# Batch normalisation over 64 tiles: the first store split in two column parts, the second store queued behind it

## The chip, the cores and the metric

The kernel runs on one core of one Trainium2 chip. The metric is the device time of one execution in microseconds (us), the median of several runs; lower is better.

## The reference

The kernel computes a batch normalisation with given (running) statistics, in float32:

```python
def setup_inputs():
    n = 32; c = 256; h = 128; w = 128
    # x: (n, c, h, w); gamma, beta, running_mean, running_var: (c,)

def reference(x, gamma, beta, running_mean, running_var):
    eps = 1e-5
    # the four parameters reshaped to (1, c, 1, 1)
    return gamma * (x - mean) / np.sqrt(var + eps) + beta
```

Per channel this is one multiplication and one addition: out = x * scale + shift, with scale = gamma / sqrt(var + eps) and shift = beta - mean * scale. The input has 537 MB and so has the output. Each element is read from HBM once and written once.

## The kernel before

**Tiles.** The 256 channels are two blocks of 128, one channel per partition. A tile is one image and one channel block: 128 partitions x 16384 columns (128 x 128 pixels) of float32, 64 KB per partition, 8.39 MB in all. There are NT = 64 tiles. SBUF holds NBUF = 3 tile buffers; tile i lives in buffer i modulo 3, is loaded into it, computed in place, and stored from it.

**Engines.** SP issues all loads, ACT issues all stores, each on its own DMA queue (q1 is SP's and q10 is ACT's in the profile). Both queues run on the core's 16 DMA engines. In every tile VectorE (DVE) computes columns 0 to 14336 (VCOLS) and ScalarE (ACT) computes the last 2048. VectorE does its share in two instructions (L132): the first covers STEP = 2560 columns, the second the rest. In tile 0 the first covers 8192 columns, since tile 0 is loaded in two halves. In the last tile VectorE stops at column 9216 (VLAST) and ACT does the remaining 7168 columns.

**Semaphores.** `early` and `loaded[s]` say that a load has landed in a buffer, `stored[s]` that a store from buffer s has landed. A DMA adds 16 when it is complete. `vdone` counts VectorE's parts (two per tile), `adone` those of ACT (one per tile).

**Order on SP.** The first half of tile 0 (L90), the four parameter rows (L93), the second half of tile 0 (L97), then tiles 1 to 63 in full (L104). Before load i, from tile 3 on, SP waits until the buffer's previous tile has been stored (L103) and until VectorE has done the first part of tile i - 1, which in turn needs load i - 1 to have landed. So apart from the first three tiles there is one load in flight at a time.

**Order on VectorE.** Scale and shift from the parameters (L91 to L127), then the two parts of each tile as it lands.

**Order on ACT.** For each tile i: wait until VectorE has done both its parts (`vdone`), wait until store i - 1 has landed, compute ACT's columns (L143), issue store i (L156), which waits for the computation. So there is one store in flight at a time. This loop is written out by hand, and ACT's instructions run in this order:

```python
for i in range(last):
    nc.scalar.wait_ge(vdone, 2 * (i + 1))
    inst = scalar_part(i, VCOLS)
    if i:
        inst._wait_ge(stored[(i - 1) % NBUF], 16 * ((i - 1) // NBUF + 1))
    store(i)
```

The last tile is computed as soon as it lands and stored without a wait for the store before it.

Of the kernel before, what the change touches and what calls it, by code (L numbers as in the profile page):

```python
# [8 lines left out]
NBUF = 3  # L9
# [2 lines left out]

STEP = 2560
VCOLS = 14336
VLAST = 9216


@with_exitstack
def kernel(
    ctx: ExitStack,  # L20
    tc: tile.TileContext,
    x: bass.AP,
    gamma: bass.AP,
    beta: bass.AP,
    running_mean: bass.AP,
    running_var: bass.AP,
    out: bass.AP,
):
    nc = tc.nc
    eps = 1e-5  # L30
    f32 = mybir.dt.float32

    N, C, H, W = x.shape
    P = nc.NUM_PARTITIONS
    assert C % P == 0
    NCB = C // P
    HW = H * W
    NT = N * NCB
    B = 32
    NQ = P // B  # L40
    NE = 16
    NPAR = 4

    xr = x.rearrange("n (cb p) h w -> (n cb) p (h w)", p=P)
    outr = out.rearrange("n (cb p) h w -> (n cb) p (h w)", p=P)

    params = ctx.enter_context(tc.tile_pool(name="params", bufs=1))
    data = ctx.enter_context(tc.tile_pool(name="data", bufs=1))
    params.tile([P, PAD], f32, name="pad", tag="pad")
    bufs = [data.tile([P, HW], f32, name=f"t{s}", tag=f"t{s}") for s in range(NBUF)]  # L50
    rows = params.tile([B, NPAR * C], f32, name="rows", tag="rows")
    turned = params.tile([B, NPAR * C], f32, name="turned", tag="turned")
    par = params.tile([P, NPAR, NCB], f32, name="par", tag="par")
    eps_t = params.tile([P, 1], f32, name="eps_t", tag="eps")
    std_t = params.tile([P, NCB], f32, name="std_t", tag="std")
    rstd_t = params.tile([P, NCB], f32, name="rstd_t", tag="rstd")
    scale_t = params.tile([P, NCB], f32, name="scale_t", tag="scale")
    ms_t = params.tile([P, NCB], f32, name="ms_t", tag="ms")
    shift_t = params.tile([P, NCB], f32, name="shift_t", tag="shift")

    loaded = [tc.alloc_semaphore(f"loaded{s}") for s in range(NBUF)]
    stored = [tc.alloc_semaphore(f"stored{s}") for s in range(NBUF)]
    early = tc.alloc_semaphore("early")
    vdone = tc.alloc_semaphore("vdone")
    adone = tc.alloc_semaphore("adone")
    fetched = tc.alloc_semaphore("fetched")
    vec = tc.alloc_semaphore("vec")
    act = tc.alloc_semaphore("act")  # L70

    with tc.tile_critical():  # L72
        count = [0]

        def step(inst, sem=None, value=None):

            if sem is not None:
                inst._wait_ge(sem, value)
            elif count[0]:
                inst._wait_ge(vec, count[0])  # L80
            inst.then_inc(vec, 1)
            count[0] += 1
            return count[0]

        left, right = slice(0, HW // 2), slice(HW // 2, HW)
        last = NT - 1

        nc.sync.dma_start(out=bufs[0][:, left], in_=xr[0][:, left]).then_inc(early, 16)  # L90
        zeroed = step(nc.vector.memset(rows[:], 0.0))  # L91
        for r, ap in enumerate((running_var, gamma, beta, running_mean)):
            inst = nc.sync.dma_start(out=rows[0:NE, r * C : (r + 1) * C], in_=ap.partition_broadcast(NE))  # L93
            if r == 0:
                inst._wait_ge(vec, zeroed)
            inst.then_inc(fetched, 16)
        nc.sync.dma_start(out=bufs[0][:, right], in_=xr[0][:, right]).then_inc(loaded[0], 16)  # L97
        for i in range(1, NT):
            s, turn = i % NBUF, i // NBUF


            if turn:
                nc.sync.wait_ge(stored[s], 16 * turn)  # L103
            inst = nc.sync.dma_start(out=bufs[s][:], in_=xr[i]).then_inc(loaded[s], 16)  # L104
            if turn:
                inst._wait_ge(vdone, 2 * (i - 1) + 1)


        step(nc.vector.memset(eps_t[:], eps))  # L109
        step(nc.vector.transpose(out=turned[:], in_=rows[:]), fetched, 16 * NPAR)  # L110

        blocks = turned.rearrange("p (rc q b) -> p rc q b", q=NQ, b=B)
        flat = par.rearrange("p r cb -> p (r cb)")
        for q in range(NQ):
            placed = step(nc.vector.tensor_copy(out=flat[q * B : (q + 1) * B], in_=blocks[:, :, q, 0]))  # L115
        var_t, gamma_t, beta_t, mean_t = (par[:, r] for r in range(NPAR))
        nc.scalar.activation(  # L117
            out=std_t[:],
            in_=var_t,
            func=mybir.ActivationFunctionType.Sqrt,  # L120
            bias=eps_t[:],
            scale=1.0,
        )._wait_ge(vec, placed).then_inc(act, 1)
        step(nc.vector.reciprocal(out=rstd_t[:], in_=std_t[:]), act, 1)  # L124
        step(nc.vector.tensor_mul(out=scale_t[:], in0=gamma_t, in1=rstd_t[:]))  # L125
        step(nc.vector.tensor_mul(out=ms_t[:], in0=mean_t, in1=scale_t[:]))  # L126
        ready = step(nc.vector.tensor_sub(out=shift_t[:], in0=beta_t, in1=ms_t[:]))  # L127
        nc.vector.wait_ge(vec, ready)

        def vector_part(i, first, end):  # L130
            t, cb = bufs[i % NBUF], i % NCB
            return nc.vector.tensor_scalar(  # L132
                out=t[:, first:end],
                in0=t[:, first:end],
                scalar1=scale_t[:, cb : cb + 1],
                scalar2=shift_t[:, cb : cb + 1],
                op0=mybir.AluOpType.mult,
                op1=mybir.AluOpType.add,
            ).then_inc(vdone, 1)

        def scalar_part(i, first):
            t, cb = bufs[i % NBUF], i % NCB
            return nc.scalar.activation(  # L143
                out=t[:, first:],
                in_=t[:, first:],
                func=mybir.ActivationFunctionType.Identity,
                bias=shift_t[:, cb : cb + 1],
                scale=scale_t[:, cb : cb + 1],
            ).then_inc(adone, 1)

        def landed(i):
            return loaded[i % NBUF], 16 * (i // NBUF + 1)

        def store(i):
            s = i % NBUF
            nc.scalar.dma_start(out=outr[i], in_=bufs[s][:])._wait_ge(adone, i + 1).then_inc(stored[s], 16)  # L156

        vector_part(0, 0, HW // 2)._wait_ge(early, 16)
        vector_part(0, HW // 2, VCOLS)._wait_ge(*landed(0))
        for i in range(1, NT):  # L160
            vector_part(i, 0, STEP)._wait_ge(*landed(i))
            vector_part(i, STEP, VLAST if i == last else VCOLS)
        for i in range(last):
            nc.scalar.wait_ge(vdone, 2 * (i + 1))
            inst = scalar_part(i, VCOLS)
            if i:
                inst._wait_ge(stored[(i - 1) % NBUF], 16 * ((i - 1) // NBUF + 1))
            store(i)
        scalar_part(last, VLAST)._wait_ge(*landed(last))
        nc.scalar.wait_ge(vdone, 2 * NT)  # L170
        store(last)

        for s in range(NBUF):
            nc.sync.wait_ge(stored[s], 16 * ((NT - s + NBUF - 1) // NBUF))
# [30 lines left out]
```

## Time and profile before

| what | value |
|---|---|
| median of 3 runs | 2482.92 us (2482.25 to 2483.06) |
| the profiled execution's own time | 2482.82 us |
| its span, from the first to the last instruction | 2481.0 us |
| moved by DMA | 1073.85 MB, mean 433 GB/s over the span |
| VectorE parts of 2560 columns (L132) | mean 1.61 us |
| ACT's part of a tile (L143, 2048 columns) | mean 2.09 us |
| load, from issue to landing (L104) | median 37.0 us |
| store, from issue to landing (L156) | median 36.5 us |
| first landing: load 1, load 2 | 55.55 us, 86.94 us |
| store 0: issued, landed | 29.06 us, 72.42 us |

The profile is one execution, recorded by the hardware profiler. "Span" is the time between the first and the last instruction; all times within it are counted from its start. L132 is line 132 of the kernel before. A row of instructions names the line, the engine, the operation and the tile that it writes and reads; "[43.38 <-DMA out_dram<-t]" says that the engine stood idle for 43.38 us before it and that a store ended this. In the waits, "a <- b: total, times, longest" says how long a waited for b. The DMA view counts packets by the time at which they begin, by queue; a packet of a full tile is one row of 64 KB. The share of a short window can be above 100% as whole packets are counted where they begin.

### The profile page before, as it was taken

How to read it: one execution, taken by the hardware profiler on the slowest of the kernel's cores; microseconds unless marked ns; L12 is line 12 of the kernel's file. 1: busy time of each engine (PE TensorE's matmuls, PEld its weight loads, DVE VectorE, ACT ScalarE, POOL GpSimd, SP SyncE). 2: the span in 40 equal slices, each digit the busy share in tenths (PEclk: the TensorE clock that was granted, in tenths of full speed). 3: DMA queues.
4: the chain of work that ended last, by engine and by line, in shares of the span. 5: the costliest groups of instructions: out<-in, count | busy, mean ns of one | idle time of the engine just before them, and what ended most of it. 6: DMA issues, size and time to landing. Idle time of an engine off the chain costs nothing.

```text
span 2481.0 us, 516 instructions
## 1 busy us (share of the span) xinstructions
DVE 508.8 (21%) x139; ACT 139.8 (6%) x66; POOL 0.2 (0%) x4
## 2 busy tenths in 40 slices
DVE  2122121221212212122121221212212122121120
ACT  0000000000000000000000000000000000000001
POOL 0000000000000000000000000000000000000000
DMA  9999999999999999999999999999999999999999
GB/s 411 435 440 428 433 440 432 430 440 432 430 440 437 427 438 436 428 437 436 432 433 438 430 434 437 432 432 437 434 431 436 437 428 437 437 428 435 437 432 402
DMA packets 18708, 1073.85 MB, mean 433 GB/s; under 512 B 2128, under 2 KB 2192, under 8 KB 2192
## 3 DMA queue, kind: packets, MB, share of 16 engines
q1 hardware_dynamic: 9488, 536.94, 50.0%
q10 hardware_dynamic: 9216, 536.88, 49.9%
q14 instruction: 4, 0.03, 0.0%
HBM read 536.94 MB, written 536.87 MB: 433 GB/s over the span
## 4 chain that ended last, share of the span: by engine, by line
DMA 92%; DVE 4%; another core or an unknown queue 2%; ACT 0%; issue 0%; SPq 0%; DVEq 0%
DMA t<-in_x_dram 92%; DVE t L132 4%; ACT t L143 0%; SPq L93 0%; DVE rows L91 0%; DVE eps_t L109 0%; DVEq L200 0%; SPq L72 0%
## 5 line engine op out<-in xcount | busy, mean ns | idle before, releaser
L132 DVE TENSOR_SCALAR t<-t,scale_t,shift_t 128x11776 f32<-128x11776 f32 (+2 forms) x128 | 505.3, 3989 | 1928.8 <-DMA t<-in_x_dram 1928.7
L143 ACT ACTIVATE t<-t,shift_t,scale_t 128x2048 f32<-128x2048 f32 x64 | 138.2, 2159 | 2297.8 <-DMA out_dram<-t 2274.9
L110 DVE STREAM_TRANSPOSE turned<-rows 32x1024 f32<-32x1024 f32 x1 | 1.2, 1232 | 11.8 <-DMA rows<-in_running_mean_dram 11.8
L117 ACT ACT_TABLE_LOAD x1 | 1.3, 1283 | 0.9 <-SPq L72 0.9
L91 DVE MEMSET rows<- 32x1024 f32 x1 | 0.9, 912 | 1.2 <-SPq L72 1.2
L117 ACT ACTIVATE std_t<-par,eps_t 128x2 f32<-128x2 f32 x1 | 0.3, 295 | 14.0 <-DVE par L115 14.0
L115 DVE COPY par<-turned 32x8 f32<-32x8 f32 x4 | 0.6, 162 | 0.1
L124 DVE RECIPROCAL rstd_t<-std_t 128x2 f32<-128x2 f32 x1 | 0.2, 166 | 0.4 <-ACT std_t L117 0.4
L125 DVE TENSOR_TENSOR scale_t<-par,rstd_t 128x2 f32<-128x2 f32 x1 | 0.2, 162 | 0.0
L127 DVE TENSOR_TENSOR shift_t<-par,ms_t 128x2 f32<-128x2 f32 x1 | 0.2, 162 | 0.0
L126 DVE TENSOR_TENSOR ms_t<-par,scale_t 128x2 f32<-128x2 f32 x1 | 0.2, 160 | 0.0
L189 POOL MEMSET const-bfloat16-1.0<- 128x1 bf16 x1 | 0.1, 101 | 0.0
L189 POOL MEMSET const-uint8-127<- 128x1 uint8 x1 | 0.1, 101 | 0.0
L189 POOL MEMSET const-float32-0.0<- 128x1 f32 x1 | 0.1, 98 | 0.2 <-issue 0.2
L189 POOL MEMSET const-float32-1.0<- 128x1 f32 x1 | 0.1, 98 | 0.0
L109 DVE MEMSET eps_t<- 128x1 f32 x1 | 0.1, 59 | 0.1
## 6 DMA issues: line engine op xcount, KB each, us to landing
t<-in_x_dram SPq DMA_DIRECT2D x2, 4096.0 KB, 15.9
out_dram<-t ACTq DMA_DIRECT2D x64, 36.5
t<-in_x_dram SPq DMA_DIRECT2D x63, 37.0
rows<-in_running_var_dram SPq DMA_DIRECT2D x1, 16.0 KB, 11.1
rows<-in_gamma_dram SPq DMA_DIRECT2D x1, 16.0 KB, 10.9
rows<-in_beta_dram SPq DMA_DIRECT2D x1, 16.0 KB, 10.7
rows<-in_running_mean_dram SPq DMA_DIRECT2D x1, 16.0 KB, 10.6
```

The costliest lines, as they stand in the source:

```text
L91: zeroed = step(nc.vector.memset(rows[:], 0.0))
L109: step(nc.vector.memset(eps_t[:], eps))
L110: step(nc.vector.transpose(out=turned[:], in_=rows[:]), fetched, 16 * NPAR)
L115: placed = step(nc.vector.tensor_copy(out=flat[q * B : (q + 1) * B], in_=blocks[:, :, q, 0]))
L117: nc.scalar.activation(out=std_t[:], in_=var_t, func=mybir.ActivationFunctionType.Sqrt, bias=eps_t[:], scale=1.0,)._wait_ge(vec, placed).t ...
L124: step(nc.vector.reciprocal(out=rstd_t[:], in_=std_t[:]), act, 1)
L125: step(nc.vector.tensor_mul(out=scale_t[:], in0=gamma_t, in1=rstd_t[:]))
L126: step(nc.vector.tensor_mul(out=ms_t[:], in0=mean_t, in1=scale_t[:]))
L127: ready = step(nc.vector.tensor_sub(out=shift_t[:], in0=beta_t, in1=ms_t[:]))
L132: return nc.vector.tensor_scalar(out=t[:, first:end], in0=t[:, first:end], scalar1=scale_t[:, cb : cb + 1], scalar2=shift_t[:, cb : cb + 1 ...
L143: return nc.scalar.activation(out=t[:, first:], in_=t[:, first:], func=mybir.ActivationFunctionType.Identity, bias=shift_t[:, cb : cb + 1] ...
L189: nc = _bacc.Bacc("TRN2", target_bir_lowering=False, num_devices=1)
```

## The change

The store of tile 0 becomes two DMAs. Columns 0 to 2048 are stored as soon as VectorE's first instruction (columns 0 to 8192 of tile 0) is done; the other 14336 columns are stored where the whole tile was stored before, after ACT's part. The early DMA has its own semaphore, `opened`, and is issued by ACT ahead of its first part. SP waits for it before it loads tile 3 into the same buffer. ACT's part of tile 1 no longer waits for store 0 to land, so that store 1 may be queued while store 0 is still in flight. From tile 2 on nothing is changed.

```diff
+FIRST = 2048
...
+    opened = tc.alloc_semaphore("opened")
...
+            if i == NBUF:
+                nc.sync.wait_ge(opened, 16)
             if turn:
                 nc.sync.wait_ge(stored[s], 16 * turn)
             inst = nc.sync.dma_start(out=bufs[s][:], in_=xr[i]).then_inc(loaded[s], 16)
...
         def store(i):
             s = i % NBUF
-            nc.scalar.dma_start(out=outr[i], in_=bufs[s][:])._wait_ge(adone, i + 1).then_inc(stored[s], 16)
+            cols = slice(0 if i else FIRST, HW)
+            nc.scalar.dma_start(out=outr[i][:, cols], in_=bufs[s][:, cols])._wait_ge(adone, i + 1).then_inc(stored[s], 16)
...
+        nc.scalar.dma_start(out=outr[0][:, :FIRST], in_=bufs[0][:, :FIRST])._wait_ge(vdone, 1).then_inc(opened, 16)
         for i in range(last):
             nc.scalar.wait_ge(vdone, 2 * (i + 1))
             inst = scalar_part(i, VCOLS)
-            if i:
+            if i > 1:
                 inst._wait_ge(stored[(i - 1) % NBUF], 16 * ((i - 1) // NBUF + 1))
             store(i)
```

## The prediction

> **What bounds the kernel now.** First the page: busy shares and queues. Columns of the queue rows: packets, MB, share of the 16 DMA engines' time.
>
> ```profile
> span 2481.0 us, 516 instructions
> DVE 508.8 (21%) x139; ACT 139.8 (6%) x66; POOL 0.2 (0%) x4
> ...
> q1 hardware_dynamic: 9488, 536.94, 50.0%
> q10 hardware_dynamic: 9216, 536.88, 49.9%
> ```
>
> No engine is near busy; the loads (q1, issued by SP) and the stores (q10, issued by ACT) together fill the 16 DMA engines. Next, stretches of the span (start:end, length, busy times, clock, DMA share, GB/s):
>
> ```profile
> 0.00:1.95 1.95, 0.73 (x1) 1.05 (x1) 0.20 (x4) 1.00 0.00 0
> ...
> 60.00:2440.00 2380.00, 487.57 (x123) 129.73 (x62) 0.00 (x0) 1.00 1.00 434
> ...
> 2479.40:2481.00 1.60, 0.00 (x0) 0.00 (x0) 0.00 (x0) 1.00 0.00 0
> ```
>
> From 1.95 to 2479.4 us the engines never stand still. 1073.85 MB at the 434 GB/s of the middle are 2474 us, so out of 2481.0 only 7 us are anything else: 1.95 before the first packet, 1.6 after the last, some 3 of start-up. **Nothing that reorders these transfers can win more than that.** The question is only whether the new order keeps the engines full.
>
> That is read from the order of packets. A load or a full store is 128 rows of 64 KB, 8 on each engine. Three short windows of the DMA view, 83.6 to 93.2, 93.2 to 107.8 and 107.8 to 117.3 us:
>
> ```profile
> q10 hardware_dynamic: 64, 4.19, 100.8%
> q1 hardware_dynamic: 16, 0.00, 0.1%
> ...
> q1 hardware_dynamic: 48, 3.15, 49.7%
> q10 hardware_dynamic: 48, 3.15, 49.7%
> ...
> q1 hardware_dynamic: 64, 4.19, 101.8%
> q10 hardware_dynamic: 16, 0.00, 0.1%
> ```
>
> When both queues hold work each engine takes one packet of each in turn; the pair of a load and a store (16 packets per engine) comes round every 38.65 us (SP issues load 3 at 88.60 and load 4 at 127.30), so one turn is 2.415 us. Between two loads there is a hole, in which 4 store packets run (first window), and between two stores one in which 4 load packets run (third). The 16 tiny packets are the completion marks: a mark is a packet too and waits for its turn. The two holes lie apart, so each is filled by the other queue. **This phase is what the change touches.** Why there are holes is in the waits and in the timeline at the start:
>
> ```profile
> ACT t L143 <- DMA out_dram<-t: 2274.9, 62, 43.4
> ...
> SPq L103 <- DMA out_dram<-t: 1395.7, 61, 67.0
> SPq L104 <- DVE t L132: 984.6, 61, 16.3
> ...
> 17.35 4.55 DVE L132 TENSOR_SCALAR t<-t,scale_t,shift_t 128x8192 f32<-128x8192 f32 x1
> ...
> 26.94 2.09 ACT L143 ACTIVATE t<-t,shift_t,scale_t 128x2048 f32<-128x2048 f32 x1 [10.49 <-DVE t L132]
> 29.06 0.38 ACTq L156 DMA_DIRECT2D out_dram<-t  x1
> ...
> 72.42 2.09 ACT L143 ACTIVATE t<-t,shift_t,scale_t 128x2048 f32<-128x2048 f32 x1 [43.38 <-DMA out_dram<-t]
> 74.54 0.34 ACTq L156 DMA_DIRECT2D out_dram<-t  x1
> ```
>
> Store i+1 is issued 2.12 us after store i has landed; load i+1 about 1.65 us after load i has landed (the first VectorE part, mean 1.61 us).
>
> **The change part by part.**
> (1) The early store. VectorE's first part ends at 17.35 + 4.55 = 21.90, so ACT issues the 2048 columns at about 21.94 (a 0.03 us handover, as before 26.94). ACT had nothing to do until 26.94, so 0.38 us of issue cost nothing. Bytes are the same; one more DMA is one more mark per engine, nothing.
> (2) But 2048 columns are 8 KB per row: 8 packets per engine of 0.30 us (2.415/8) each. A turn each means that the first 1 MB takes as many turns as 8 MB do, with a 2.4 us load packet between any two. The other 14336 columns (2.11 us a packet), issued at 29.06 as before, stand behind them in the same rings. So store 0 needs 16 turns in place of 8, and loads 1 and 2 (16 turns as well) run through beside it: load 1 lands near 45 instead of 55.55, load 2 near 80 instead of 86.94, store 0 near 82 instead of 72.42: 22.7 + 16 x 2.415 + 8 x 0.30 + 8 x 2.11 = 80.6, and about 1 us of start-up of the store queue. The early store makes the stores late.
> (3) The second store does not wait for the first: tile 1 is ready at 45 + 7.94 + 2.12 = 55, so store 1 stands behind store 0 and starts at about 82 without a hole. That hole would have been filled by load packets anyway.
> (4) SP's new wait for the early store, ahead of load 3 with all later loads behind it: the store has landed by about 48 and SP waits for the rest of store 0 until 82 anyway. Nothing; only if those 1 MB came after the rest would it cost.
> (5) The tail: after the last load there must be enough store left to cover 6.36 us of ACT and the issue. In the new order store 62 covers that as well. Nothing.
>
> **The sum hangs on load 3.** It now waits for store 0 (near 82), at the moment when store 1 begins, in place of coming 14 us after store 1 was issued. A DMA issued into busy engines takes about 1 us to reach them and then lets the packet already chosen go first (store 1: issued 74.54, first packet 78.8 to 79.3). So store 1 gets 2 packets alone if load 3 arrives within its first turn, 3 if within the second. With 2, the other 6 alternate with 6 load packets, and 2 load packets are left for the next store hole. The hole is one turn for the mark, 0.4 landing, 2.12 ACT and issue, 0.95 to 1.2 to reach the engines: 5.9 to 6.1 us. Two load packets cover 4.83, so all engines idle 1.05 to 1.3 us. The load after it is issued some 1.9 us behind that store, so the store again gets 2 packets: **it repeats every period.** With 3, the load has 3 packets (7.2 us) left and nothing idles.
> How much a start from empty engines adds, no row in the middle shows: at the very start the first packets took up to 0.5 us longer than the later ones, so 0 to 0.55. Per period 1.05 to 1.85, I take 1.45, halfway: 61 stores x 1.45 = 88 us (64 to 113).
> Which is it, 2 or 3? Load 3 waits for store 0 AND load 2. On an engine that gets its first early-store packet after one packet of load 1 instead of two, a store packet more lies before the end of load 2: load 2 then lands 2 us later (all engines must finish), load 3 comes 1.7 us later, store 1 gets 3. Rows for it, packets beginning in 29.5 to 30.2 and in 30.2 to 30.4, and then, a turn later, 31.9 to 33.4 us:
>
> ```profile
> q1 hardware_dynamic: 12, 0.79, 259.9%
> ...
> q1 hardware_dynamic: 4, 0.26, 348.6%
> ...
> q1 hardware_dynamic: 13, 0.85, 179.3%
> q10 hardware_dynamic: 3, 0.20, 30.2%
> ```
>
> Store 0, issued at 29.06, went straight into 3 of 16 engines, those whose packet began at 30.28 or later (1.22 us after the issue); one at 30.15 (1.09) had chosen before. In the new kernel the issue is at 21.94 and the latest engines begin load 1 at 23.04 to 23.09, 1.10 to 1.15 us after it. The limit is somewhere in 1.09 to 1.22: above 1.15 none is caught, a little over half of that stretch.
> The Trainium skill (DMA: Bandwidth & Descriptors, Queues, rings and completion order) says that an engine drains a whole packet of about 9 to 17 descriptors from one queue before it switches. By that rule the eight 8 KB rows would pass in one turn, no delay would arise, and the sum would be 0. The rows above show one 64 KB row, and even one 4-byte mark, per turn; small rows side by side no run here shows.
>
> **The rivals.**
> A (forecast): 2 packets, idle in every period: 2482.8 (the profiled execution, 1.8 over its span, 0.1 under the median) + 88 = 2571, its own range 2547 to 2596. Chance 0.53; another 0.03 for worse.
> B: an engine is caught and the phase has 3 load packets left: 2483, within 1 us, no idle. For it: the limit may lie below 1.15. Against it: its cover of 7.2 us over a hole of 6 leaves about 1 us, and the packets that begin together within 0.5 us at 80 us are spread over 2.3 us by the end, so it may tip over into A part of the way. 0.27. This is the case on the other side: it decides from a start of the early store 0.05 us sooner.
> C: small packets are taken several per turn: the stores are then ahead of before and the holes stay apart, 2483. For it: nothing shows 8 KB packets; against: the marks. 0.14.
> D: faster by filling the start: at most the 3 us of start-up, 2480, which is below 0.2% (5 us; about what a measurement of this kernel tells from no change). Over 0.2% faster has no place to come from: 0.03.
>
> **How the numbers follow.** Slower by over 0.2%: 0.53 + 0.03 = 0.56; within: 0.27 + 0.14 = 0.41; faster 0.03. The time is A's, 2571. B and C hold 0.41, so the range reaches down to them: 2481 to 2592.
>
> **What would show it.** Of (2): in the DMA view from 27 to 44 us, q10 packets of 8 KB spread one per turn, load 1 landing near 45 and store 0 near 82. Of A: ACT's period at L143/L147 about 40 us in place of 38.65, DMA share under 1.00 in the middle, load 4 landing 2 us behind store 2. B: a period of 38.65 with loads landing about 5 us after stores. Store 0 landing before 72 would prove C and the reasoning of (2) wrong; faster than 2478, that the engines were not full before.

## The result, and the profile after

The changed kernel takes 2596.74 us (median of 6 runs, 2592.65 to 2610.88) against 2482.99 us before (6 runs, 2481.96 to 2484.78): 113.75 us more. The ratio of the means is 1.0465 (95% interval 1.0440 to 1.0489): slower by 4.65%. Medians and ranges are of all runs; a ratio here leaves out runs that lie over 1.5% above the fastest of the same kernel, of which this kernel has none. The profiled execution took 2600.65 us, its span is 2598.9 us.

First the start, from the timeline of the kernel after (start, duration, engine, line, operation; in brackets what the engine waited for):

```profile
17.36 4.55 DVE L136 TENSOR_SCALAR t<-t,scale_t,shift_t 128x8192 f32<-128x8192 f32 x1
21.94 0.38 ACTq L168 DMA_DIRECT2D out_dram<-t  x1
...
29.20 0.34 ACTq L161 DMA_DIRECT2D out_dram<-t  x1
45.62 7.94 DVE L136 TENSOR_SCALAR t<-t,scale_t,shift_t 128x2560 f32<-128x2560 f32 x2 [18.58 <-DMA t<-in_x_dram]
...
55.72 0.34 ACTq L161 DMA_DIRECT2D out_dram<-t  x1
88.11 7.93 DVE L136 TENSOR_SCALAR t<-t,scale_t,shift_t 128x2560 f32<-128x2560 f32 x2 [34.55 <-DMA t<-in_x_dram]
122.68 2.09 ACT L147 ACTIVATE t<-t,shift_t,scale_t 128x2048 f32<-128x2048 f32 x1 [67.00 <-DMA out_dram<-t]
124.81 0.34 ACTq L161 DMA_DIRECT2D out_dram<-t  x1
```

The early store is issued at 21.94. Load 1 lands at 45.6 (before: 55.55), load 2 at 88.1 (before: 86.94). The next rows say when store 0 has landed: its two parts are listed with their time from issue to landing.

```profile
out_dram<-t ACTq DMA_DIRECT2D x1, 7168.0 KB, 59.1
out_dram<-t ACTq DMA_DIRECT2D x1, 1024.0 KB, 25.7
```

The early 1 MB need 25.7 us and are there at 47.6; the other 7 MB land at 29.20 + 59.1 = 88.3, 16 us later than the whole store before. Why, the DMA view shows for 27 to 44 us (packets, MB, share):

```profile
q1 hardware_dynamic: 96, 6.29, 85.5%
q10 hardware_dynamic: 101, 0.83, 11.5%
```

For 96 load packets 101 store packets ran, so the queues did take turns packet by packet, but the stores moved 0.83 MB in their turns and the loads 6.29.

From there the loss comes in every period, and the page hides it: the DMA row of its 40 slices still shows a 9 everywhere. The rate tells it, here for 500 to 2400 us of the kernel after (columns as in the stretches above, DMA share and GB/s last):

```profile
500.00:2400.00 1900.00, 368.80 (x94) 98.35 (x47) 0.00 (x0) 1.00 0.99 414
```

Before it was 434 GB/s in the middle. The engines are "busy" 99% of the time and move 5% less, so packets take longer. Which ones: the timeline of one store hole (the stretch between two stores in which only load packets run), and the DMA view from 2476.0 to 2478.4 and from 2479.4 to 2481.8 us, both windows as long as a turn:

```profile
2473.07 2.09 ACT L147 ACTIVATE t<-t,shift_t,scale_t 128x2048 f32<-128x2048 f32 x1 [37.69 <-DMA out_dram<-t]
2475.19 0.34 ACTq L161 DMA_DIRECT2D out_dram<-t  x1
2477.91 7.93 DVE L136 TENSOR_SCALAR t<-t,scale_t,shift_t 128x2560 f32<-128x2560 f32 x2 [33.66 <-DMA t<-in_x_dram]
2479.55 0.33 SPq L108 DMA_DIRECT2D t<-in_x_dram  x1
```

```profile
q10 hardware_dynamic: 16, 1.05, 135.5%
q1 hardware_dynamic: 16, 0.00, 0.4%
...
q10 hardware_dynamic: 16, 1.05, 100.8%
```

The store is issued 4.4 us ahead of the next load. When it comes, the last load packet is already running on every engine (they begin from 2474.1 to 2475.1). Its first 16 packets take 1.355 x 2.4 = 3.25 us each in place of 2.42. No engine counts as idle for this; it is inside the packets. In other periods there is a true gap as well, here between two stretches of the same kernel:

```profile
2429.00:2434.60 5.60, 0.00 (x0) 1.31 (x1) 0.00 (x0) 1.00 0.87 375
2434.60:2436.00 1.40, 0.00 (x0) 0.78 (x1) 0.00 (x0) 1.00 0.00 0
2436.00:2474.60 38.60, 7.93 (x2) 1.53 (x1) 0.00 (x0) 1.00 1.02 421
```

From 2434.6 to 2436.0 us no data packet begins, while ACT computes its 2.09 us (issue at 2435.41); 14 of the 16 engines stand empty for 1.2 to 1.95 us, to about 2436.3. The period, taken between the starts of ACT's parts, was 38.67 us on average before and is 40.51 now. Of 59 periods, 41 end without a gap, at 39.84 on average, and 18 with one, at 41.84. Over 61 stores, 61 x (40.51 - 38.67) = 112 us: nearly the whole loss of 114.

Counted per engine from the packets of the trace (a packet is put down to the engine whose packet before ends where it begins), the store hole holds 3 load packets, in periods with a gap (3.1 on average) as in those without (3.1); before there were 4 in the prediction's window and up to 6 later. Between 300 and 2350 us it is 3 in 662 of 800 cases, and the hole of the loads has 3 store packets in 672 of 800. The difference is in how far the engines have drifted apart. A store has landed when its last engine is done. In the 18 periods with a gap that engine ends its part 3.2 us behind the middle one on average, in the 41 without 1.1 us, and the others run out of loads meanwhile.

That the two holes have moved together is in SP's waits: it waits for the store first, then for VectorE.

```profile
SPq L107 <- DMA out_dram<-t: 2128.9, 61, 82.8
SPq L108 <- DVE t L136: 362.3, 61, 6.5
```

Before a load was released, SP waited on average 984.6 / 61 = 16.1 us for VectorE after the store had landed; now it is 362.3 / 61 = 5.9 us. This distance measures how far a load's hole follows a store's hole, and it is used below to compare all kernels.

### The profile page after: what moved, and what is told of

It is laid out like the page before. It is cut to its first block, busy times and chain, and to the rows that moved or that the text cites. A ratio compares the mean times of both kernels' runs of the same rounds, so it can differ in the third digit from the quotient of the medians.

```text
span 2598.9 us, 516 instructions
## 1 busy us (share of the span) xinstructions
DVE 508.8 (20%) x139; ACT 139.8 (5%) x66; POOL 0.2 (0%) x4
## 4 chain that ended last, share of the span: by engine, by line
DMA 93%; DVE 4%; another core or an unknown queue 1%; ACT 0%; issue 0%; SPq 0%; DVEq 0%
DMA t<-in_x_dram 93%; DVE t L136 4%; ACT t L147 0%; SPq L95 0%; DVE rows L93 0%; SPq L99 0%; DVE eps_t L113 0%; DVEq L206 0%; SPq L74 0%
## 6 DMA issues: line engine op xcount, KB each, us to landing
out_dram<-t ACTq DMA_DIRECT2D x1, 7168.0 KB, 59.1
out_dram<-t ACTq DMA_DIRECT2D x1, 1024.0 KB, 25.7
```

## The experiments

The theory: nothing that was changed costs time by itself. The start sets how the loads' hole and the stores' hole lie to each other, and since each queue has one transfer in flight, this phase is kept to the end. The rivals: the small packets cost, the added wait costs, or the queued second store does.

**The changed kernel with load 3 held back once.** VectorE runs eight memsets of an unused tile between its two parts of tile 2, and SP waits for them before load 3 (LATE is 8).

```diff
...
             if i == NBUF:
                 nc.sync.wait_ge(opened, 16)
+                nc.sync.wait_ge(late, LATE)
...
             vector_part(i, 0, STEP)._wait_ge(*landed(i))
+            for n in range(LATE if i == NBUF - 1 else 0):
+                inst = nc.vector.memset(rows[:], 0.0)
+                if n:
+                    inst._wait_ge(late, n)
+                inst.then_inc(late, 1)
```

> The changed kernel with load 3 alone held back once, by eight memsets of 0.91 us between VectorE's two parts of tile 2 (about 7.5 us, some three turns of 2.415 us). Phase theory (the loss comes from where the hole of the loads and the hole of the stores lie to each other, and the start only sets this): store 1 gets 5 to 6 packets alone, 4 load packets fill each store hole from then on, and 61 periods of 38.65 us follow: 2481 to 2486 us. Rival (the split store, its small packets or SP's added wait cost the time themselves): all of these are still there, so 2597 us or, with 7 us of delay more, 2604.

Measured: 2483.49 us (10 runs), ratio to before 1.0017 (0.9986 to 1.0049). A single delay of 9.4 us (load 3 is issued 11.1 us after load 2 has landed in place of 1.65, and so 9.0 us after store 0 has landed in place of 1.5) takes the whole loss away, with the split store, the small packets, the queued store and SP's wait all still there. SP's waits:

```profile
SPq L111 <- DVE t L139: 1259.2, 60, 21.6
SPq L110 <- DMA out_dram<-t: 1038.8, 60, 18.1
```

The load's hole now follows the store's by 1259.2 / 60 = 21.0 us. Two of the ten executions took 2518 and 2525 us; they have no profile, and what happened in them is not known.

**The kernel before with store 1 held back once.** ACT copies an unused tile seven times ahead of the issue of store 1 (LATE is 7).

```diff
...
+            for n in range(LATE if i == 1 else 0):
+                inst = nc.scalar.activation(out=rows[:], in_=turned[:], func=mybir.ActivationFunctionType.Identity, bias=shift_t[:B, 0:1], scale=scale_t[:B, 0:1])
+                if n:
+                    inst._wait_ge(late, n)
+                inst.then_inc(late, 1)
             store(i)
```

> The kernel before with store 1 alone held back once, by seven copies of about 1 us each on ACT ahead of its issue (about 7 us). No split, no queued store, no added wait on SP. Phase theory: load 3 then arrives within the first or second turn of store 1, as in the changed kernel, and each store hole is covered by 2 or 3 load packets: 2580 to 2610 us, over 95 us slower for a delay of 7 us. Rival (the parts of the change cost the time): a delay of 7 us behind which load 2 keeps the engines full costs at most 7 us: 2483 to 2490.

Measured: 2596.35 us, ratio 1.0458 (1.0443 to 1.0474). Its timeline at the place, and SP's waits:

```profile
74.50 8.86 ACT L171 ACTIVATE rows<-turned,shift_t,scale_t 32x1024 f32<-32x1024 f32 x7
82.13 0.34 ACTq L158 DMA_DIRECT2D out_dram<-t  x1
82.16 7.94 DVE L134 TENSOR_SCALAR t<-t,scale_t,shift_t 128x2560 f32<-128x2560 f32 x2 [18.74 <-DMA t<-in_x_dram]
83.80 42.65 SPq L106 DMA_DIRECT2D t<-in_x_dram  x2
```

```profile
SPq L105 <- DMA out_dram<-t: 2137.5, 61, 67.1
SPq L106 <- DVE t L134: 348.0, 61, 11.3
```

The store was held back 7.6 us (82.13 in place of 74.54), and 114 us were lost: the loss of the change without any of its parts. 348.0 / 61 = 5.7 us between the holes, as in the changed kernel.

**The same with twelve copies.**

> The kernel before with store 1 held back once by twelve copies on ACT, about 13 us, in place of seven. Phase theory: store 1 then comes after load 3, as in the kernel with the early store alone, 2 packets of cover on both sides and idle engines in both holes: 2640 to 2730 us. Rival (the loss grows with the delay that is put in): 13/7.6 of the 114 us of the shorter delay, 2695 at most and with no plateau, or 2490 if the engines stay full.

Measured: 2719.58 us, ratio 1.0955 (1.0939 to 1.0972), at the upper end of the range and above the 2695 us that the rival allowed at most. The store was held back 13.9 us (88.40 in place of 74.54). Now store 1 comes behind load 3 (83.69), and SP waits for VectorE only once in the whole run; the store's landing releases the load and the next store alike.

**The two parts of the change, each alone.** The early store with the wait for store 0 put back (`if i:`), and the queued store with tile 0 stored whole (`if i > 1:` in the kernel before).

> The early store alone: ACT's part of tile 1 waits for store 0 again, as before. Phase theory: store 1 is then issued at about the same time as load 3, 2 us after store 0 has landed, the two holes fall together, each with about 2 packets of cover: slower than the changed kernel, 2600 to 2650 us. Rival (the second store queued behind the first does the harm): back at 2483.

> The queued second store alone: the first store is whole again, ACT's part of tile 1 doesn't wait for it. Phase theory: the stores gain the one hole, some 4 turns, on the loads; 4 load packets still fill each later store hole: 2482 to 2486 us. Rival (the second store queued behind the first does the harm): near 2597.

Measured: the early store alone 2722.07 us, ratio 1.0959 (1.0936 to 1.0982), above the range expected. The queued store alone 2496.11 us over 10 runs, ratio 1.0043 (1.0028 to 1.0059): two executions at 2482.5 and eight from 2494.6 to 2498.4. So the early store does the harm, and the queued second store takes half of it back; by the theory because store 1 then runs in the place where the two holes would have fallen together. In the early store alone they do: load 3 is issued at 81.74, just as store 0 has landed (81.67), only 2 load packets lie in every store hole between 300 and 2350 us, and the middle runs at 395 GB/s with a DMA share of 0.95:

```profile
500.00:2400.00 1900.00, 357.10 (x90) 94.24 (x45) 0.00 (x0) 1.00 0.95 395
```

**The queued store once more**, for a profile of an execution near 2496 us.

> The kernel with the queued second store alone once more, for a profile of one of its executions near 2496 us (8 of 10 lay there, 2 at 2482.5). Phase theory: the 14 us are either a single stretch in which the holes have drifted together, or the last store, which begins late because the stores ahead of it are done too early: in either case the middle runs at 38.65 us a period. Rival: a loss of 0.2 us in every period.

Measured: 2497.67 us, its profile has a span of 2494.8 us. The expectation was wrong: the middle doesn't run at the full rate, but at 432 GB/s from 60 to 2400 us against 434 before, which is 2340 x (1 - 432/434) = 11 us, spread over the periods as some 0.2 us each. Another 2 us are lost ahead of the last store. The 0.2 us lie in the loads: between 300 and 2350 us 437 load packets took over 2.6 us and no store packet did, and no engine stood empty. SP waits 1875.0 / 61 = 30.7 us for VectorE here, so that in a period of 38.65 us the load's hole is already near the store's hole that comes next. Why it costs something with 4 or 5 store packets in it stays open.

**Larger early packets.** FIRST = 8192 in place of 2048: 4 MB early, 32 KB packets, the same 16 packets per engine for store 0.

> The changed kernel with 8192 columns in the early store in place of 2048 (4 MB early instead of 1 MB): its packets are 32 KB, four times as long, but store 0 still needs 16 packets per engine. Phase theory (a turn is a packet whatever its size, so store 0 ends beside load 2 as before): load 3 meets the start of store 1 again, 2590 to 2610 us. Rival (8 KB packets are too small to be moved well): four times larger packets take at least half of the 114 us away, below 2540.

Measured: 2593.53 us, ratio 1.0446 (1.0422 to 1.0471). Four times larger packets change nothing, so it isn't that small packets move badly. In its profile load 3 is issued at 83.05, 0.8 to 1.7 us after the first packets of store 1, and on all 16 engines store 1 runs 3 packets before the first of load 3.

**Fewer early packets.** The same 1 MB at the same moment, as 8192 columns of 32 partitions; the rest of tile 0 in two stores. SP waits for both that count on `opened`.

```diff
-FIRST = 2048
+FIRST = 8192
+ROWS = 32
...
-                nc.sync.wait_ge(opened, 16)
+                nc.sync.wait_ge(opened, 32)
...
+            if i == 0:
+                nc.scalar.dma_start(out=outr[0][:ROWS, FIRST:], in_=bufs[0][:ROWS, FIRST:])._wait_ge(adone, 1).then_inc(opened, 16)
+                nc.scalar.dma_start(out=outr[0][ROWS:], in_=bufs[0][ROWS:]).then_inc(stored[0], 16)
+                return
...
-        nc.scalar.dma_start(out=outr[0][:, :FIRST], in_=bufs[0][:, :FIRST])._wait_ge(vdone, 1).then_inc(opened, 16)
+        nc.scalar.dma_start(out=outr[0][:ROWS, :FIRST], in_=bufs[0][:ROWS, :FIRST])._wait_ge(vdone, 1).then_inc(opened, 16)
```

> The same 1 MB stored early at the same moment, cut otherwise: 8192 columns of 32 partitions, which are 2 packets of 32 KB per engine in place of 8 of 8 KB. The rest of tile 0 follows in two stores (8192 columns of these 32 partitions, and the other 96 partitions whole). Store 0 then needs 2 + 2 + 6 = 10 packets per engine in place of 16. Phase theory: store 0 ends before load 2 (near 75 us against 90), the holes stay apart, 2481 to 2500 us. Rival (storing early, or the queued second store, costs the time itself): 2597.

Measured: 2496.3 us, ratio 1.0051 (1.0030 to 1.0071); one of four executions took 2542 us. With 10 turns for store 0 in place of 16 nearly 9/10 of the loss is gone, though it stores as much, as early, and queues the second store as well. Together with the run before (four times the bytes in as many packets, the same loss) this says that the number of packets set the phase in the change, and not the bytes.

**Smaller delays of load 3.** The first experiment with three memsets and with one.

> The changed kernel with load 3 held back once by three memsets, about 3.6 us, one and a half turns, in place of eight (9.4 us). Phase theory: store 1 gets one to two packets more alone, 4 load packets are left for each store hole, and the loss is gone all the same: 2481 to 2500 us. If the loss went down with the size of the delay instead (a rival in which the delay makes up for something): 3.6/9.4 of it gone, about 2553.

> The same with a single memset, 1.2 us, half a turn. Phase theory: at most one packet is added to the 2 or 3 that store 1 gets alone, which isn't enough to line a store up a full packet ahead: 2560 to 2605 us, no gain or little. Rival (any delay of load 3 mends it): below 2500.

Measured, three memsets: 2485.05, 2492.02, 2586.78 and 2588.55 us, two executions on each side. One memset: five of nine executions at 2489.6 to 2491.2 us and four at 2586.6 to 2607.5. Both expectations were wrong in part: I had put each on one side. Near 2490 or near 2590 us, and here nothing in between: the same program on the same chip takes either time. (The stray executions of two other kernels, 2518, 2525 and 2542 us, do lie in between.)

Two profiles point at where it is settled. Here the execution of 2485.05 us with three memsets, and then the one of 2591.49 us with one:

```profile
79.41 1.61 DVE L139 TENSOR_SCALAR t<-t,scale_t,shift_t 128x2560 f32<-128x2560 f32 x1 [26.66 <-DMA t<-in_x_dram]
84.60 80.95 SPq L111 DMA_DIRECT2D t<-in_x_dram  x3
...
88.12 1.61 DVE L139 TENSOR_SCALAR t<-t,scale_t,shift_t 128x2560 f32<-128x2560 f32 x1 [34.91 <-DMA t<-in_x_dram]
90.95 77.59 SPq L111 DMA_DIRECT2D t<-in_x_dram  x3
```

Up to these rows the two programs are the same, and yet load 2 lands at 79.4 in one and at 88.1 in the other. In the first no engine was caught, in the prediction's sense that it begins its first early-store packet after one packet of load 1 instead of two; in the second one was. The other profiles with the start of the changed kernel agree: about 79.6 with none caught (the first experiment, the early store alone), about 88.1 with two (the change, the shorter hole below). That this decides between the two times is not shown, since the other executions have no profile.

**A shorter hole.** The start of the changed kernel, but ACT computes its part before it waits for the store, so that only the issue stands in the hole.

```diff
-            inst = scalar_part(i, VCOLS)
+            scalar_part(i, VCOLS)
             if i > 1:
-                inst._wait_ge(stored[(i - 1) % NBUF], 16 * ((i - 1) // NBUF + 1))
+                nc.scalar.wait_ge(stored[(i - 1) % NBUF], 16 * ((i - 1) // NBUF + 1))
             store(i)
```

> The changed kernel with ACT's computation moved out of the store hole: ACT computes its part of tile i as soon as VectorE is done, and only the issue waits for store i - 1. The start is that of the changed kernel. Phase theory: the store hole is shorter by ACT's 2.09 us (3.8 us in place of 5.9), so that 2 to 3 load packets suffice to cover it: 2485 to 2540 us, over half of the 114 us gone. Rival (what was changed at the start costs the time in every period, whatever the hole): 2597.

Measured: 2558.19 us (2549.59 to 2565.85), ratio 1.0304 (1.0275 to 1.0333). A third of the loss is gone where over half was expected. The store holes are filled now: 4 or 5 load packets lie in most of them, and their first store packets take 2.42 us. But with the shorter hole the stores gain on the loads. The issue of a load comes 8.9, 13.7, 18.5, 23.4, 28.2 and 32.7 us behind that of the store before it (loads 4 to 9), and then stays between 28.5 and 34.1 us to the end, near the next store's hole. There the loads pay: between 300 and 2350 us 1008 load packets took over 2.6 us and no store packet did, and over 500 to 2400 us the rate is 421 GB/s. So the length of the hole matters, but a shorter store hole moved the phase to another bad place.

All kernels together, with the distance of the holes in the profiled execution (SP's wait for VectorE ahead of a load, per load; "none" where the store's landing alone releases the loads) and its time:

| kernel | distance, us | profiled execution, us |
|---|---|---|
| early store alone | none | 2718.5 |
| before, store 1 later by 13.9 us | none | 2718.4 |
| first 8192 columns early | 342.5 / 61 = 5.6 | 2597.2 |
| before, store 1 later by 7.6 us | 348.0 / 61 = 5.7 | 2596.6 |
| the change, load 3 later by one memset | 346.1 / 60 = 5.8 | 2591.5 |
| the change | 362.3 / 61 = 5.9 | 2600.7 |
| the change, load 3 later by three memsets | 679.1 / 60 = 11.3 | 2485.1 |
| before | 984.6 / 61 = 16.1 | 2482.8 |
| the change, load 3 later by eight memsets | 1259.2 / 60 = 21.0 | 2483.6 |
| 1 MB early as 32 rows | 1278.5 / 61 = 21.0 | 2495.0 |
| queued store alone | 1569.2 / 61 = 25.7 | 2482.7 |
| queued store alone, once more | 1875.0 / 61 = 30.7 | 2496.6 |
| the change, ACT computes first | 1969.5 / 61 = 32.3 | 2556.0 |

With no distance the loss is 236 us, below 6 us it is 109 to 118, whatever made it so; from 11 to 26 us it is at most 12. Towards the end of the period of 38.65 us it rises again: 14 us at 30.7, and 73 at 32.3, there in a kernel with a shorter hole. No kernel here beats the one before: with the engines full from the first packet to the last, none could by more than the 3 us of start-up.

## Why the prediction was right and wrong

**Direction and place were right, the way there only in part.** The engines were full before; the early store's small packets take a turn each and hold store 0 back; the two holes come close together, and the loss repeats in every period. The first steps came out: issue at 21.94, early store landed at 47.6 (put at about 48), load 1 at 45.6 (put at 45). Load 2 and store 0, put at 80 and 82, landed at 88.1 and 88.3 in the profiled execution; in the early store alone they came at 79.6 and 81.7. The parts put at nothing were nothing: the first experiment keeps them all and loses nothing.

**The step that failed is the count in the hole, with the price that stands on it**: "store 1 gets 2 packets alone if load 3 arrives within its first turn", so that 2 load packets are left, all engines idle 1.05 to 1.3 us, and "it repeats every period". The runs show 3 and 3: 3 store packets alone (672 of 800 cases), 3 load packets in the store hole (662 of 800), and a gap in 18 of 59 periods only. Where load 3 was issued within the first turn of store 1, 0.8 to 1.7 us after its first packets (8192 columns early), store 1 still got 3 packets alone. So the forecast's way into the loss was not the one that was taken. The count of 3 is that of the rival, which was put at no cost; that slower came out was in part luck.

**The price of a hole**, "per period 1.05 to 1.85, I take 1.45", came out at 113.75 / 61 = 1.86, and so the time at 2596.74 in place of 2571. It is made of other parts than the sum had:

- The gap was put at 1.05 to 1.3 us in every period. Counted from 125 us on, each engine stood empty for some 28 us in all, 0.46 a period.
- The start was put at 0 to 0.55 us, from the first packets of the whole run. (In the profile before, these are packets of 32 KB that take up to 1.92 us in place of 1.21, so 0.7 longer and not 0.5.) A start from empty engines costs almost nothing: behind the 18 gaps the first store packets took 2.50 us on average. What costs are packets that take longer while all engines work. Counted over all 64 KB packets of the kernel after from 125 us on, 997 store packets took over 2.6 us, 0.77 longer than a turn on average, and 585 load packets, 0.93 longer: (997 x 0.77 + 585 x 0.93) / 16 engines = 82 us, or 1.34 us a period. No term of the sum had this.

**Which packets these are.** In the 41 periods without a gap it is the first packet of a store, with 3.19 us on average. In the 18 with a gap it is above all the third and fourth of the store (2.87 and 2.65) and the first of the load that comes in there (3.54). Why they take longer was not settled.

**The rival with 3 load packets fell by its price.** It was put at 2483, since 7.2 us of cover stand over a hole of 6. The cover did keep the engines at work in 41 of 59 periods, and still each cost 39.84 - 38.67 = 1.17 us. A store that arrives while the last load packet runs pays 0.8 us though no engine is empty. In the store holes of the kernels that lose little there are 4 load packets and more, and their first store packets take 2.42 or 2.43 us.

**The condition between the two was no good either.** It said that one engine caught by the early store one packet sooner would make load 2 land 2 us later and save the phase. In the profiled execution two of the 16 engines were caught (their first early-store packets begin at 25.50 and 25.65 us, the others from 27.5 on); load 2 landed at 88.1 us against 79.7 in the execution of the first experiment, where none was: 8 us later, four times what I had put, and store 0 with it. The 8 us lie on the two engines. Between 47 and 88 us store 0's 56 KB packets took 2.44 us on average on them and load 2's 2.95, against 2.12 and 2.43 on the other 14, though both queues held work there. The phase was no better; nor was it better with 8192 columns early, where no engine was caught.

**Small packets several per turn** (the third rival) fell with 101 store packets among 96 load packets. The Trainium skill (DMA: Bandwidth & Descriptors, Queues, rings and completion order) has an engine switch between queues packet by packet, with about 9 to 17 descriptors in a packet. The trace agrees that queues take turns by packets. That the eight 8 KB rows would share one packet, as the prediction read the rule, is not so: each took a turn of its own. How many descriptors a row has, no run here shows.

**A start so close to the edge was the right reading.** The kernels with one and three memsets fall on both sides from one execution to the next, 100 us apart. For the change itself all six runs took over 2592 us.

## What to carry to other kernels

In a kernel that is bound by DMA with one load and one store in flight, look at where the holes of the two queues lie to each other. Here each was filled by the other queue as long as a load's hole followed a store's by 11 to 26 us of a period of 38.65, and a change of a few us at the start moved them together for the whole run. A row of a partition was a turn on its engine in these runs, with 8 KB as with 64, so splitting a transfer by columns doubled its turns and made it late beside a queue of long packets. A hole that the other queue only just covers, here with 3 packets, is not free. Judge DMA by GB/s in a stretch of the middle, since the busy share stayed at 99% while packets stretched.

## What the runs showed that I had not expected

A store packet that comes when the last load packet is already running took 0.8 us longer, with its engine at work all the time (3.25 us in place of 2.42), while one that starts on an empty engine took 2.50. A few engines that lag by a turn delay the landing for all, and the others run empty meanwhile. Four-byte completion marks and 8 KB rows are given a turn like 64 KB rows. And one program on one core of one chip, with the granted clock at 1.000 throughout, took near 2490 or near 2590 us; two such profiles first differ in the order of DMA packets at the start.
